# Partition sums of the modulation values: fp32 products with one column of ones, or high and low parts in fp32r with two columns

## The chip, the cores and the metric

The kernel runs on one core of one Trainium2 chip. The metric is device time in microseconds of one execution. A version's time is the median of its runs.

## The reference, cut to what matters

The reference is two transformer blocks in a row on 512 tokens of width 1024. The first has attention (eight heads with a forget gate, eight with dilated windows) and a layer of 16384 small experts; the second has a retention branch, a convolution branch and a gated feed-forward layer. The second block is modulated by a vector `c`:

```
cs = jax.nn.silu(c)
mod = cs @ ada_w[l] + ada_b[l]                    # 1024 -> 6 * 1024
sh_m, sc_m, gt_m, sh_f, sc_f, gt_f = jnp.split(mod, N_MOD, axis=-1)
h = modulate(rmsnorm(x, norm_mix_g[l]), sh_m, sc_m)
```

The change touches only how the six vectors of 1024 values in `mod` are summed.

## The kernel before, in words

**Layout.** Activations are kept with features on the 128 partitions, as 8 chunks of 128 features by 512 tokens. Weights come from memory as fp32 chunks of 128 by 1024 (512 KB).

**Projections.** A projection chunk (`wload`, lines 140 to 147, and `mm3`, lines 149 to 153) works in three products. ACT copies the weight chunk into the format fp32r (line 145, tile `wh`, the high part), DVE or POOL subtracts that from the fp32 chunk (line 146, tile `wl`, the low part), and TensorE runs high times high, high times low and low times high (lines 151, 152, 153), each with 512 or 256 columns of activations. The tags `wh` and `wl` have three buffers each in a pool that lives through the whole kernel, so a new high part waits until TensorE is done with the chunk three before it.

**The modulation values.** `ada(j)` (line 245) makes one of the six vectors. Eight weight rows of 128 by 1024 are multiplied by a value per partition and added into the fp32 tile `acc` (name `ada`): the first on ACT (line 259), four on DVE (line 261), the last three scaled on ACT (line 263) and added on POOL (line 264). `ada_sum` (line 270) then sums over partitions: for each of 8 blocks of 128 columns, `acc` is the stationary operand and one column of fp32 ones is the moving one (line 274), the result lands in one column of the PSUM tile `adaps`, and DVE adds `ada_b` and writes `mod` (line 276). For j of 0 to 3 the sum follows at once; for j of 4 and 5 it is put off to `after` (line 368), which is called between the two halves of the output projection's last chunks (`resid`) and behind them.

**The order of the work.** In this stage no order is written out by hand: a scheduler orders each engine's instructions by the place in the program and by when it expects operands and buffers to be ready, and the engines then run that order with semaphores. The loop over `c` in `attention` emits the q and k projections of the next pair of heads, the heads of this pair (`heads`, ending in the transposes `mt` of line 449) and then `ada(c - 1)`. Behind `attention` come the queries of the expert layer (`queries`, `proj_halves`): three weight chunks of `wq` are split into high and low parts, the low ones on POOL, and their products start with the first 256 tokens, going through the three chunks for each k. From there to the end of the expert layer the order is written by hand.

Of the kernel before, what the change touches and what calls it, by code (L numbers as in the profile page):

```python
# [11 lines left out]
F32R = mybir.dt.float32r  # L12
# [3 lines left out]
AF = mybir.ActivationFunctionType  # L16
OP = mybir.AluOpType
# [3 lines left out]
D = 1024  # L21
# [37 lines left out]
def f32(ap):  # L59
    return ap.bitcast(F32)  # L60
# [39 lines left out]
class Builder:  # L100
# [113 lines left out]
    def consts(self):  # L214
        nc, a, c = self.nc, self.a, self.const
        self.hT = self.big.tile([128, KD, T], F32, name="hT")
        self.xh = self.big.tile([128, KD, T], F32R, name="xh")
        self.xl = self.big.tile([128, KD, T], F32R, name="xl")
        self.xt = self.big.tile([128, D], F32, name="xt")
        nc.vector.memset(self.xt[:, :T // 2], 0.0)  # L220
        self.blank = self.xt[:, :T // 2].bitcast(BF16)
        self.mean_w = c.tile([128, 1], F32, name="mean_w")
        nc.vector.memset(self.mean_w, 1.0 / D)
        self.vec = c.tile([128, a["vecs"].shape[1]], F32, name="vec")
        nc.scalar.dma_start(self.vec, a["vecs"])
        self.ones1 = c.tile([128, 1], F32, name="ones1")
        nc.vector.memset(self.ones1, 1.0)
        o = self.a["vec_off"]
        self.v = {n: self.vec[:, o[n]:o[n] + w] for n, w in self.a["vec_w"].items()}

# [38 lines left out]

    def ada_sum(self, j, acc):  # L270
        nc = self.nc
        p = self.bank("pt", "adaps")
        for m in range(8):
            nc.tensor.matmul(p[:, m:m + 1], lhsT=acc[:, m * 128:m * 128 + 128], rhs=self.ones1,
                             start=True, stop=True)
        nc.vector.tensor_tensor(self.mod[:, j * 8:j * 8 + 8], p[:, 0:8],
                                self.v["ada_b"][:, j * 8:j * 8 + 8], OP.add)
        if j == 5:
            self.gs = self.const.tile([128, 16], F32, name="gs")
            for i, (g, sc) in enumerate((("norm_mix_g", 1), ("norm_ffn_g", 4))):  # L280
                nc.vector.scalar_tensor_tensor(self.gs[:, i * 8:i * 8 + 8], self.mod[:, sc * 8:sc * 8 + 8], 1.0,
                                               self.v[g], op0=OP.add, op1=OP.mult)
# [1117 lines left out]
```

## Time and profile before

| What | Value |
|---|---|
| median of 3 runs | 2491.91 us (2490.35 to 2492.84) |
| the profiled execution's own time | 2493.93 us |
| span in its profile | 2492.0 us |
| TensorE busy | 2458.2 us, 99% of the span |
| VectorE (DVE) busy | 1714.6 us |
| ScalarE (ACT) busy | 938.9 us |
| GpSimd (POOL) busy | 623.3 us |
| mean granted TensorE clock | 0.995 |

The span is what the profiler sees of one execution; the execution's own time is 1.93 us longer. Matmul records overlap, because the next one starts while the last drains: the distance from one start to the next tells what a matmul takes from TensorE, not its duration. An fp32 matmul of these sums leaves two records, each with a weight load of its own; an fp32r matmul leaves one.

### The profile page before, as it was taken

The page shows a single profiled execution, that of the slowest core. Times are in us where ns is not written, and L with a number is a line of the kernel's source. Part 1 is how long each engine was busy: PE and PEld are TensorE (multiplying, and loading weights), DVE is VectorE, ACT ScalarE, POOL GpSimd, SP SyncE. Part 2 cuts the span into 40 slices and gives each one's busy share as a digit, 9 for nine tenths or more (in the row PEclk, how much of TensorE's full clock was granted, in tenths as well). Part 3 has the DMA queues.
Part 4 walks back from the last instruction along what each step waited for, and adds up shares of the span by engine and source line. Part 5 has one row for each costly group of instructions (what it writes and reads, how often), then busy time and mean ns, then how long its engine had stood idle before and what let it go on. Part 6 is the DMA issues. An engine that isn't in the chain of part 4 may idle for free.

```text
span 2492.0 us, 34252 instructions
## 1 busy us (share of the span) xinstructions
PE 2458.2 (99%) x12881; PEld 2135.9 (86%) x12881; DVE 1714.6 (69%) x3224; ACT 938.9 (38%) x1401; POOL 623.3 (25%) x460
## 2 busy tenths in 40 slices
PE   9999999999999999999999999999999999999998
PEld 7788889999999999999888887777888888888887
DVE  5767589898885998889888885877543336433333
ACT  5667244444554333333333334411223223322221
POOL 1132146670002666566543320000000001000000
PEclk9999999999999999999999999999999999999999
DMA  4476224455777999999999982422232322232332
GB/s 168 146 244 223 76 82 135 157 174 187 263 266 275 399 376 370 371 369 387 370 383 383 380 295 96 132 85 85 85 102 94 102 93 93 86 101 93 97 94 64
DMA packets 191285, 496.99 MB, mean 199 GB/s; under 512 B 16136, under 2 KB 85384, under 8 KB 189584
## 3 DMA queue, kind: packets, MB, share of 16 engines
q1 hardware_dynamic: 142352, 322.02, 38.5%
q0 software_dynamic: 36864, 134.23, 14.2%
q10 hardware_dynamic: 11904, 38.56, 4.0%
q8 instruction: 101, 1.65, 0.3%
q14 instruction: 64, 0.52, 0.1%
HBM read 455.48 MB, written 39.27 MB: 199 GB/s over the span
## 4 chain that ended last, share of the span: by engine, by line
PE 94%; DVE 2%; ACT 2%; DMA 1%; issue 0%; ACTq 0%; SPq 0%; POOL 0%; DVEq 0%
PE up L151 7%; PE up L153 7%; PE up L152 7%; PE oacc L966 7%; PE oacc L965 7%; PE oacc L964 7%; PE fg L152 2%; PE fg L153 2%; PE fg L151 2%; PE fd L151 2%; PE fd L153 2%; PE fd L152 2%; PE q L151 2%; PE q L152 2%; PE fu L152 2%; PE fu L151 2%
## 5 line engine op out<-in xcount | busy, mean ns | idle before, releaser
L145 ACT ACTIVATE wh<-ws 128x1024 fp32r<-128x1024 f32 (+2 forms) x206 | 214.7, 1043 | 659.7 <-issue 228.5
L146 DVE TENSOR_TENSOR wl<-ws,wh 128x1024 fp32r<-128x1024 f32 (+2 forms) x200 | 240.8, 1204 | 254.6 <-ACT wh L145 253.1
L884 ACT ACTIVATE wh<-ws 128x1024 fp32r<-128x1024 f32 x269 | 284.5, 1058 | 227.6 <-issue 78.2
L888 DVE TENSOR_TENSOR wl<-ws,wh 128x1024 fp32r<-128x1024 f32 x231 | 285.7, 1237 | 105.3 <-ACT wh L884 102.7
L151 PE MATMUL up<-xh,wh 128*128 128x384 f32 x1024 | 346.6, 338 | 1.3 <-ACT gel L918 1.3
L153 PE MATMUL up<-xh,wl 128*128 128x384 f32 x1024 | 343.8, 336 | 0.3 <-DVE wl L888 0.3
L152 PE MATMUL up<-xl,wh 128*128 128x384 f32 x1024 | 343.3, 335 | 0.0
L966 PE MATMUL oacc<-wh,al 128*128 128x512 f32 x768 | 300.1, 391 | 0.0
L965 PE MATMUL oacc<-wl,ah 128*128 128x512 f32 x768 | 300.0, 391 | 0.0
L964 PE MATMUL oacc<-wh,ah 128*128 128x512 f32 x768 | 299.2, 390 | 0.0
L970 POOL DMA_INDIRECT row<-in_peer_u,eidx x128 | 182.6, 1427 | 324.4 <-DMA ws<-in_u_blk 195.2
L970 POOL DMA_INDIRECT row<-in_peer_v,eidx x128 | 188.1, 1470 | 210.3 <-DVE acc L996 189.0
L918 ACT ACTIVATE gel<-up 128x384 f32<-128x384 f32 x128 | 63.0, 492 | 409.3 <-PE up L153 409.3
L151 PEld LDWEIGHTS up<-xh,wh 128*128 128x128 f32 x1024 | 192.7, 188 | 3.6 <-ACT gel L918 1.6
L152 PEld LDWEIGHTS up<-xl,wh 128*128 128x128 f32 x1024 | 192.9, 188 | 2.0
L153 PEld LDWEIGHTS up<-xh,wl 128*128 128x128 f32 x1024 | 192.7, 188 | 0.9 <-DVE wl L888 0.6
L966 PEld LDWEIGHTS oacc<-wh,al 128*128 128x128 f32 x768 | 144.1, 188 | 29.8
L965 PEld LDWEIGHTS oacc<-wl,ah 128*128 128x128 f32 x768 | 144.1, 188 | 29.0
L964 PEld LDWEIGHTS oacc<-wh,ah 128*128 128x128 f32 x768 | 144.2, 188 | 28.5
L996 DVE SCALAR_TENSOR_TENSOR acc<-row,wg,acc 128x1024 f32<-128x1024 f32 x127 | 162.5, 1280 | 1.0
L985 DVE CUSTOM_DVE_ANT_0 scr<-row,xt 128x1024 bf16<-128x1024 f32 x128 | 156.3, 1221 | 5.5 <-DMA row<-in_peer_u,eidx 3.7
L146 POOL TENSOR_TENSOR wl<-ws,wh 128x1024 fp32r<-128x1024 f32 x6 | 14.4, 2402 | 567.8 <-ACT wh L145 567.8
(375 smaller groups left out, 5329.2 us busy)
## 6 DMA issues: line engine op xcount, KB each, us to landing
ws<-in_u_blk SPq DMA_DIRECT2D x128, 512.0 KB, 3.9
ws<-in_v_blk SPq DMA_DIRECT2D x128, 512.0 KB, 9.2
ws<-in_w_t SPq DMA_DIRECT2D x64, 512.0 KB, 3.3
ws<-in_ada_w SPq DMA_DIRECT2D x48, 512.0 KB, 4.6
gates_d<-gst ACTq DMA_DIRECT2D x12, 2048.0 KB, 7.0
gr<-gates_d SPq DMA_DIRECT2D x32, 768.0 KB, 10.6
gel_d<-gel ACTq DMA_DIRECT2D x61, 192.0 KB, 2.8
gel<-gel_d SPq DMA_DIRECT2D x61, 192.0 KB, 8.1
```

The costliest lines, as they stand in the source:

```text
L145: nc.scalar.activation(wh, ws, AF.Copy)
L146: (low or nc.vector).tensor_tensor(wl, ws, f32(wh), OP.subtract)
L151: mm(out, lhsT=wh, rhs=xh, start=first, stop=False)
L152: mm(out, lhsT=wh, rhs=xl, start=False, stop=False)
L153: mm(out, lhsT=wl, rhs=xh, start=False, stop=last)
L884: self.nc.scalar.activation(x["wh"], x["ws"], AF.Copy)
L888: eng.tensor_tensor(x["wl"], x["ws"], f32(x["wh"]), OP.subtract)
L964: mm(o, lhsT=ah[:, t], rhs=vh[:, d], start=j == 0, stop=False)
L965: mm(o, lhsT=ah[:, t], rhs=vl[:, d], start=False, stop=False)
L966: mm(o, lhsT=al[:, t], rhs=vh[:, d], start=False, stop=j == 127)
L970: self.nc.gpsimd.indirect_dma_start(out=u, out_offset=None, in_=self.a["peer_v" if i >= 128 else "peer_u"], in_offset=bass.IndirectOffsetO ...
L996: nc.vector.scalar_tensor_tensor(self.acc, u, self.wg[:, j:j + 1], self.acc, op0=OP.mult, op1=OP.add)
```

## The change

A tile `ones2` of 128 by 2 in fp32r is made once from the fp32 ones. `ada_sum` splits `acc` into a high part on ACT (a buffer of the tag `wh`) and a low part on DVE (a buffer of the tag `wl`), and for each of the 8 blocks runs two matmuls, high and low, each with two columns of ones, that accumulate in PSUM. The PSUM tile has two columns for each block, of which the first is read.

```diff
         self.ones1 = c.tile([128, 1], F32, name="ones1")
         nc.vector.memset(self.ones1, 1.0)
+        self.ones2 = c.tile([128, 2], F32R, name="ones2")
+        nc.scalar.activation(self.ones2, self.ones1.to_broadcast([128, 2]), AF.Copy)
...
     def ada_sum(self, j, acc):
         nc = self.nc
-        p = self.bank("pt", "adaps")
+        p = self.bank("pt", "adaps", (128, 8, 2))
+        hi = self.w.tile([128, D], F32R, tag="wh", bufs=3, name="wh")
+        nc.scalar.activation(hi, acc, AF.Copy)
+        lo = self.w.tile([128, D], F32R, tag="wl", bufs=3, name="wl")
+        nc.vector.tensor_tensor(lo, acc, f32(hi), OP.subtract)
         for m in range(8):
-            nc.tensor.matmul(p[:, m:m + 1], lhsT=acc[:, m * 128:m * 128 + 128], rhs=self.ones1,
-                             start=True, stop=True)
-        nc.vector.tensor_tensor(self.mod[:, j * 8:j * 8 + 8], p[:, 0:8],
+            for x in (hi, lo):
+                nc.tensor.matmul(p[:, m], lhsT=x[:, m * 128:m * 128 + 128], rhs=self.ones2,
+                                 start=x is hi, stop=x is lo)
+        nc.vector.tensor_tensor(self.mod[:, j * 8:j * 8 + 8], p[:, :, 0],
                                 self.v["ada_b"][:, j * 8:j * 8 + 8], OP.add)
```

## Rows read from the trace of the kernel before

**Rows 1.** The page: busy time, and the chain that ended last, by engine.

```profile
PE 2458.2 (99%) x12881; PEld 2135.9 (86%) x12881; DVE 1714.6 (69%) x3224; ACT 938.9 (38%) x1401; POOL 623.3 (25%) x460
...
PE 94%; DVE 2%; ACT 2%; DMA 1%; issue 0%; ACTq 0%; SPq 0%; POOL 0%; DVEq 0%
```

**Rows 2.** By tile, adaps: the sums' weight loads, ns min/median/max, first and last start.

```profile
L274 PEld LDWEIGHTS adaps<-ones,ada x96: 190/192/192, 122.5 to 300.4; 128*128 128x128 f32 x96
```

**Rows 3.** By tile, mod: its reader in the norms of the second block.

```profile
L294 ACT ACTIVATE xh<-y,mod x32: 492/496/511, 1525.5 to 2127.6; 128x256 fp32r<-128x256 f32 x32
```

**Rows 4.** Timeline of PE around the first sum: start, us, operation.

```profile
122.58 1.84 PE L274 MATMUL adaps<-ones,ada 128*128 128x1 f32 x16
124.28 0.48 PE L152 MATMUL q<-xl,wh 128*128 128x512 f32 x1
124.60 0.39 PE L153 MATMUL q<-xh,wl 128*128 128x512 f32 x1
124.83 0.40 PE L151 MATMUL q<-xh,wh 128*128 128x512 f32 x1
```

**Rows 5.** Stretches: busy of PE, PEld, DVE, ACT, POOL; clock, DMA share, GB/s.

```profile
300.00:305.00 5.00, 5.00 (x32) 5.00 (x32) 4.25 (x19) 1.57 (x4) 2.72 (x3) 0.66 0.44 131
80.00:240.00 160.00, 152.74 (x938) 129.16 (x937) 114.38 (x238) 108.98 (x227) 49.20 (x30) 0.99 0.68 225
```

**Rows 6.** Timeline of PE at the end of the output projection, and the queries' start.

```profile
289.71 0.28 PE L153 MATMUL res<-mixh,wlast 128*128 128x256 f32 x1
289.83 1.84 PE L274 MATMUL adaps<-ones,ada 128*128 128x1 f32 x16
291.54 0.36 PE L151 MATMUL res<-mixh,wlast 128*128 128x256 f32 x1
...
298.86 1.84 PE L274 MATMUL adaps<-ones,ada 128*128 128x1 f32 x16
300.57 0.58 PE L92 MATMUL st<-mean_w,sq 128*128 128x1 f32 x4
301.01 0.36 PE L151 MATMUL q<-xh,wh 128*128 128x256 f32 x1
```

**Rows 7.** Timeline of ACT at the start, where the new constant joins.

```profile
4.30 0.21 ACT L250 ACTIVATE cs<-vec 128x8 f32<-128x8 f32 x1 [1.83 <-DMA vec<-in_vecs]
```

**Rows 8.** Timeline of PE: fp16 products of 128 columns, later in the kernel.

```profile
603.23 0.22 PE L803 MATMUL gp<-o,o 128*128 128x128 f16 x1
603.29 0.22 PE L802 MATMUL gp<-o,o 128*128 128x128 f16 x1
```

**Rows 9.** Groups by line, 80 to 240 us: count, busy us, mean ns, idle before.

```profile
L146 DVE TENSOR_TENSOR wl<-ws,wh 128x1024 fp32r<-128x1024 f32 x13 | 15.9, 1222 | 0.2 <-ACT wh L145 0.2
L145 ACT ACTIVATE wh<-ws 128x1024 fp32r<-128x1024 f32 x13 | 13.5, 1047 | 0.0
...
L151 PEld LDWEIGHTS q<-xh,wh 128*128 128x128 f32 x48 | 9.1, 189 | 3.4 <-ACT ks L397 1.7 <-ACT wh L145 0.4
...
L424 PEld LDWEIGHTS <-identb 128*128 128x128 bf16 x31 | 3.3, 105 | 2.6 <-issue 1.8
```

**Rows 10.** Timeline of POOL: an add for the first sum, a later weight split.

```profile
113.48 2.38 POOL L264 TENSOR_TENSOR ada<-ada,ws 128x1024 f32<-128x1024 f32 x1
...
283.56 2.40 POOL L146 TENSOR_TENSOR wl<-ws,wh 128x1024 fp32r<-128x1024 f32 x1 [3.04 <-ACT wh L145]
```

**Rows 11.** Timeline of ACT: idle behind the first sum; copies of the queries' weights.

```profile
127.77 0.59 ACT L389 ACTIVATE qh<-q 64x512 fp32r<-64x512 f32 x1 [4.39 <-PE q L153]
...
271.59 1.06 ACT L145 ACTIVATE wh<-ws 128x1024 fp32r<-128x1024 f32 x1 [3.90 <-issue]
...
282.42 1.06 ACT L145 ACTIVATE wh<-ws 128x1024 fp32r<-128x1024 f32 x1 [3.80 <-PE res L152]
```

**Rows 12.** Timeline of PE: products of the queries behind the last sum.

```profile
301.73 0.41 PE L152 MATMUL q<-xl,wh 128*128 128x256 f32 x1
301.95 0.41 PE L153 MATMUL q<-xh,wl 128*128 128x256 f32 x1
```

## The prediction

> **What bounds the kernel now.** The page comes first: TensorE is busy for 2458.2 of 2492.0 us and holds 94% of the chain that ended last [rows 1]. So a step costs or gives time only through what TensorE itself does, or through a wait of TensorE that nothing else fills. By tile, the sums have 96 records, two for each of 48 fp32 matmuls, each with its weight load, in six groups from 122.5 to 300.4 us [rows 2]. The timeline of TensorE tells what one group takes: in the tail of the attention stage it starts at 289.83 and the next product at 291.54, so 1.71 us, or 0.107 us a record [rows 6]; at 122.58 it is 1.70 [rows 4]. All six are 10.3 us. No reader hurries: the norms of the second block read `mod` from 1525.5 us on [rows 3]. The stretch from 80 to 240 us, with the heads of attention and the first four sums, shows TensorE busy for 152.74 of 160 us, DVE for 114.38, ACT for 108.98 [rows 5]: it has 7.3 us of waits and some slack beside it. [...]
>
> **The constant.** One ACT operation on 128 by 2 elements, like the 0.21 us one on 128 by 8, which itself came after 1.83 us of waiting for a DMA [rows 7]. That wait hides it: 0, at most +0.2.
>
> **The matmuls.** 48 fp32 matmuls with two records each become 96 fp32r matmuls with one record each: the count of weight loads is the same. With one or two columns there is nothing to stream, so I take the load as what paces them, at 0.107 us as now: 0. No row has fp32r below 256 columns, so the price is bounded. At the 0.12 us of fp32r with 256 columns [rows 6], 16 times 0.013 for six groups is +1.2. At the 0.06 us of fp16 products [rows 8], a group takes 0.96, and six save 4.5. If a short fp32r product ran in two passes as fp32 does, 32 records of 0.107 are 3.42 a group, +10.3 in all. I stay at 0, because a load in fp32r is recorded with 189 ns, near the 192 of fp32 [rows 2] and far from the 105 of bf16 [rows 9]. Behind an fp32 group the second fp32r product starts 0.32 us after the first, not 0.23 [rows 4]: 0.09 for the change of format. Four groups stand behind transposes of fp32 data, where this only moves; one has fp32r on both sides: -0.1, between -0.5 and 0.
>
> **The splits of the first four sums.** Each adds a copy on ACT (1047 ns) and a subtraction on DVE (1222 ns) [rows 9]: 4.2 and 4.9 us, 9.1 if nothing hid them. The matmuls now wait for the low part, and behind them in TensorE's order stand q products; behind the copy on ACT the next head's `qh`, behind the subtraction on DVE the next `ada` and `ql`. But the first sum's last POOL add ends at 115.9 [rows 10] and its matmuls start at 122.58 [rows 4]: 6.7 us for 2.3 us of splitting. ACT then idles 4.39 us before `qh` [rows 11]. What fails to hide I take from the stage's own leak: 7.3 of 160 us is 4.6%, and 4.6% of 9.1 is +0.4. Both ends: +9.1, and -1.5 if the order, which the scheduler makes anew, happens to close some of the 7.3 us of waits. If this cover is gone, TensorE is late with q and k, and then with the next scores. SP issues no new DMA; POOL's own operations are unchanged.
>
> **The splits of the last two sums.** Here the buffers decide. `wh` has three. In the tail ACT takes one each time TensorE finishes a chunk: the three query chunks are copied from 271.59 to 282.42, the first and last of three [rows 11]. In program order the parts for j = 4 and 5 come before the query chunks, so they should take the buffers at 271.6 and 277, and keep them until their matmuls are done: 291.5 and 300.6 [rows 6]. The first query chunk is then copied at 282.4, the second at 291.6, the third at 300.6. That one is ready in its low part at about 300.6 + 1.06 + 2.40 [rows 10, 11] = 304.1, or some 0.8 later behind POOL's norm work, while the products start at 301.01 [rows 6] and reach the third chunk six products later, about 302.3, its low part at 302.7 (0.22 each [rows 12]). In strict order TensorE waits 1.4 to 2.2 us; if the scheduler runs the other two chunks first, 48 products cover it. I take +0.8. Upper end: 2.2 and one more stretch at the lower clock, which costs 5 times 0.34, or 1.7, by the granted clock of 300 to 305 us [rows 5]: +3.9. Lower end: the stretch at the lower clock goes, because the last sum moves away from `st`: -1.7. The POOL queue is the one moved: its subtraction lands among the norm's.
>
> **The sum.** 0 - 0.1 + 0.4 + 0.8 = +1.1 us on the profiled execution's 2493.93 (span 2492.0 and 1.93 around it): 2495.0. That execution lies 2.0 above the median of the runs shown, so on the median 2491.91 I give **2493.0 us**. A measurement of this kernel can tell about 0.2%, 5 us, from no change; this is no change.
>
> **The rivals.**
>
> *The short product in two passes* (slower). Place: TensorE, all six groups. It costs +10.3 beyond my sum, 2503.3. It decides from a group length of about 2.4 us on (six times 0.7 is over 4). For it: no row shows fp32r below 256 columns, so none speaks of such a short product. Against it: every fp32r product here has one record. Chance 0.08.
>
> *The splits stay on the chain of the heads* (slower): the low part is late at all four sums, TensorE stands still behind it, and the scores after it move; up to +9.1 in place of +0.4, 2501.7, and over 5 from about half of that on. For it: DVE is 71% busy there. Against it: 6.7 us of lead. Chance 0.10.
>
> *The query chunks wait for the sums' buffers in strict order*: +3.9 in place of 0.8, 2496.1, still no change. For it: three buffers and the program's order. Against it: 48 products to run first. Chance 0.14.
>
> *A fast load* (faster): the fp32r loads go at 0.06 and save 4.5, so 2488.5; with the low stretch gone as well, 2486.8. For it: the fp16 rows. Against it: 189 ns against 105 [rows 9]. Chance 0.08, half of it faster by over 5 us. [...]
>
> **How the numbers follow.** The main case has 0.60, its own bounds 2489 to 2497. Faster by over 5 us: half of the fast load and a little of the main case's low end, 0.07. Slower by over 5: the two passes 0.08, the heads 0.09, the tail and a bad order 0.04: 0.21. The rest, 0.72, is no change. The range runs from 2488.0 (the fast load with the splits) to 2500.0 (the heads half exposed); above it lie the two passes and the worst of the heads, below it a fast load with luck.
>
> **What the new profile would show.** Right: `adaps` as 96 records of two columns, a group still 1.7 to 1.9 us; copies for j = 4 and 5 on ACT near 272 and 277, and the second and third query chunks copied near 292 and 301; TensorE's busy share from 80 to 240 us within a microsecond of 152.74. Wrong: groups of 3.4 or of 1.0 us; idle time of TensorE before `adaps` ended by the low part; query copies still in front of 283; the clock of 300 to 305 us back at 1.0, or a second low stretch.

## The result, and the profile after

The changed kernel takes **2505.01 us** (median of six runs, 2502.54 to 2508.37) against 2492.35 for the kernel before (six runs, 2490.35 to 2493.93): ratio 1.0053 [1.0043, 1.0063], slower by 12.7 us. The prediction was 2493.0, and its range ended at 2500.0. The profiled execution is the slowest of the six (2508.37, span 2506.3), so its stretches add up to 14.3 us, 1.6 more than the medians differ by.

The page of the kernel after, busy time and the chain by engine:

```profile
PE 2463.0 (98%) x12881; PEld 2140.8 (85%) x12881; DVE 1720.5 (69%) x3230; ACT 945.7 (38%) x1409; POOL 617.8 (25%) x460
...
PE 93%; DVE 2%; ACT 2%; DMA 1%; issue 1%; POOL 1%; SPq 0%; ACTq 0%; DVEq 0%; POOLq 0%
```

Next to [rows 1] TensorE has the same 12881 instructions and is busy 4.8 us longer, and the span grew by 14.3: most of the loss is idle time, the rest is the same work done more slowly. First the suspects of the prediction. By tile, the loads of the sums after (ns min/median/max, first and last start):

```profile
L281 PEld LDWEIGHTS adaps<-ones,wh x48: 190/192/333, 122.6 to 311.7; 128*128 128x128 f32 x48
L281 PEld LDWEIGHTS adaps<-ones,wl x48: 192/192/333, 122.7 to 311.8; 128*128 128x128 f32 x48
```

96 loads at a median of 192 ns, as in [rows 2]. TensorE's timeline after, around the group of the sum for j = 4:

```profile
300.25 0.17 PE L281 MATMUL adaps<-ones,wh 128*128 128x2 f32 x1
...
301.96 0.36 PE L151 MATMUL res<-mixh,wlast 128*128 128x256 f32 x1
302.16 0.28 PE L152 MATMUL res<-mixl,wlast 128*128 128x256 f32 x1
```

From the group's start to the next product it is 1.71 us, as before [rows 6]. The matmuls cost what the old ones cost, and the loss is elsewhere. To place it I used two landmarks of TensorE's timeline: the transposes `mt` that end each head, and the spread of `half`, which ends the tail of the attention stage (starts in us). From here on "head" followed by a number is one turn of the loop over `c`, which holds a pair of heads; turns 4 to 7 are the dilated ones.

| landmark | before | after | moved by |
|---|---|---|---|
| `mt`, head 0 | 109.28 | 109.24 | 0.0 |
| `mt`, head 2 | 147.50 | 148.41 | 0.9 |
| `mt`, head 3 | 174.47 | 178.93 | 4.5 |
| `mt`, head 4 | 196.62 | 204.57 | 8.0 |
| `mt`, head 7 | 254.94 | 264.43 | 9.5 |
| spread of `half` | 311.20 | 324.77 | 13.6 |
| end of the span | 2492.0 | 2506.3 | 14.3 |

So there are two losses: **9.5 us in the heads** (head 0 to head 7: 145.66 us before, 155.19 after) and **4.1 us in the tail** (head 7 to the spread: 56.26 before, 60.34 after). The landmark of head 7 is not a clean cut, because products of the output projection are mixed in before it: behind it stand 120 products `res` of 512 columns before and 124 after (rows of lines 151 to 153), 0.23 us each. So 0.9 us of the tail's 4.1 is work that has only changed sides, and the losses are nearer to 10.4 and 3.2. The stretches after (columns as in [rows 5]):

```profile
80.00:240.00 160.00, 147.66 (x876) 125.10 (x875) 110.70 (x220) 102.97 (x207) 44.88 (x29) 0.96 0.62 209
```

TensorE is busy for 147.66 us where [rows 5] has 152.74, and its mean granted clock is 0.96 instead of 0.99.

**The heads.** The timeline of the engines around the second sum (j = 1) after, start and duration in us, in brackets the idle time and what ended it:

```profile
135.96 4.82 POOL L266 TENSOR_TENSOR ada<-ada,ws 128x1024 f32<-128x1024 f32 x2
...
138.26 0.19 ACT L437 ACTIVATION_READ_ACCUMULATOR e<-e,m 128x1 f32 x1
...
140.81 1.06 ACT L276 ACTIVATE wh<-ada 128x1024 fp32r<-128x1024 f32 x1 [2.37 <-POOL ada L266]
...
141.78 0.47 ACT L445 ACTIVATE pts<-pt 128x384 f32<-128x384 f32 x1
...
142.30 1.44 PE L447 MATMUL o<-v,pts 128*128 128x64 f32 x11 [2.05 <-ACT pts L445]
```

The new copy (L276) stands on ACT between an exponential of head 2 and that head's next `pts`. ACT has nothing to do from 138.4 on, but the copy at the head of its queue waits for POOL's last addition, which ends at 140.78. Behind the copy waits `pts`, and behind `pts` TensorE: 2.05 us. ACT keeps to its order here: the 0.47 us copy of `pts` starts at 141.78, behind the new one of 140.81, though the last transposes `pt` before it had ended by 139.65. At the third sum the same happens:

```profile
162.09 4.83 POOL L266 TENSOR_TENSOR ada<-ada,ws 128x1024 f32<-128x1024 f32 x2
...
166.95 1.06 ACT L276 ACTIVATE wh<-ada 128x1024 fp32r<-128x1024 f32 x1 [2.46 <-POOL ada L266]
...
168.66 0.90 PE L440 MATMUL pt<-ident,e 128*128 128x128 f32 x3 [2.15 <-ACT e L437]
```

A third stall has another cause. TensorE's timeline at the first scores of head 5, and the waits from 100 to 330 us (total, times, longest, in us), both after:

```profile
200.90 0.38 PE L428 MATMUL s<-ks,qh 128*128 128x256 f32 x1 [1.51 <-DVE m L435]
```

```profile
ACT wh L145 <- PE adaps L281: 6.7, 2, 4.3
ACT wh L276 <- POOL ada L266: 5.4, 3, 2.5
...
DVE e L435 <- DMA bias<-in_k_dil: 2.3, 1, 2.3
```

There VectorE waited for the bias of a dilated head, which SP issued only at about 195 us, behind two `ada_w` loads. And behind the second and the third of these stalls TensorE's clock falls (stretches of 4 us, columns as in [rows 5]):

```profile
168.00:172.00 4.00, 3.34 (x17) 3.34 (x18) 3.63 (x7) 3.44 (x9) 0.00 (x0) 0.58 0.59 199
172.00:176.00 4.00, 4.00 (x21) 3.81 (x21) 1.16 (x6) 3.20 (x7) 0.00 (x0) 0.57 0.60 190
200.00:204.00 4.00, 3.10 (x16) 2.74 (x17) 3.29 (x6) 1.54 (x3) 0.00 (x0) 0.85 0.10 24
204.00:208.00 4.00, 4.00 (x24) 3.66 (x24) 0.89 (x3) 0.60 (x1) 0.00 (x0) 0.73 0.93 373
```

In the kernel before every stretch of 4 us from 100 to 300 us has 1.00. These four lose 4 times (0.42 + 0.43 + 0.15 + 0.27) = 5.1 us of full clock. With the stalls, 2.05 + 2.15 + 1.51 = 5.7, that makes 10.8 at most (a stall inside one of these stretches is counted twice), enough for the 9.5 to 10.4.

**The tail.** ACT's timeline after, the copies alone:

```profile
282.01 1.06 ACT L276 ACTIVATE wh<-ada 128x1024 fp32r<-128x1024 f32 x1 [3.91 <-PE res L152]
...
287.45 1.06 ACT L276 ACTIVATE wh<-ada 128x1024 fp32r<-128x1024 f32 x1 [3.86 <-PE res L152]
...
292.83 1.06 ACT L145 ACTIVATE wh<-ws 128x1024 fp32r<-128x1024 f32 x1 [3.79 <-PE res L152]
...
302.02 1.06 ACT L145 ACTIVATE wh<-ws 128x1024 fp32r<-128x1024 f32 x1 [4.26 <-PE adaps L281]
...
312.01 1.06 ACT L145 ACTIVATE wh<-ws 128x1024 fp32r<-128x1024 f32 x1 [2.42 <-PE adaps L281]
```

The parts for j = 4 and 5 take two of the three `wh` buffers, and the query chunks, which were copied by 282.42 before [rows 11], come at 292.83, 302.02 and 312.01. TensorE's timeline shows the two waits that this ends in:

```profile
307.80 0.43 PE L210 MATMUL spread<-ident,n 128*128 128x128 f32 x2 [1.09 <-DVE n L201]
...
314.04 0.60 PE L92 MATMUL st<-mean_w,sq 128*128 128x1 f32 x4 [1.95 <-ACT sq L86]
```

The second is ACT's queue again: `sq` stands behind the query copy of 312.01, which waited for `adaps`. The first is VectorE, whose operations stretched while POOL made the low parts of these late chunks. The timelines of POOL and of DVE after:

```profile
303.16 2.39 POOL L146 TENSOR_TENSOR wl<-ws,wh 128x1024 fp32r<-128x1024 f32 x1 [6.79 <-ACT wh L145]
...
313.14 2.37 POOL L146 TENSOR_TENSOR wl<-ws,wh 128x1024 fp32r<-128x1024 f32 x1 [2.73 <-ACT wh L145]
```

```profile
304.33 1.25 DVE L195 TENSOR_SCALAR n<-n 128x2 int32<-128x2 int32 x1
...
313.40 2.39 DVE L309 TENSOR_TENSOR xl<-y,xh 128x256 fp32r<-128x256 f32 x1 [1.11 <-ACT xh L307]
...
316.88 0.41 DVE L309 TENSOR_TENSOR xl<-y,xh 128x256 fp32r<-128x256 f32 x1
317.22 0.16 DVE L195 TENSOR_SCALAR n<-n 128x2 int32<-128x2 int32 x1
```

The operations that take 0.16 and 0.41 us later take 1.25 and 2.39 here, and they end at 305.58 and 315.79, where POOL's end at 305.55 and 315.51.

### The profile page after: what moved, and what is told of

Its sections match the earlier page's. It is cut to its first block, busy times and chain, and to the rows that moved or that the text cites. A ratio compares the mean times of both kernels' runs of the same rounds, so it can differ in the third digit from the quotient of the medians.

```text
span 2506.3 us, 34260 instructions
## 1 busy us (share of the span) xinstructions
PE 2463.0 (98%) x12881; PEld 2140.8 (85%) x12881; DVE 1720.5 (69%) x3230; ACT 945.7 (38%) x1409; POOL 617.8 (25%) x460
## 4 chain that ended last, share of the span: by engine, by line
PE 93%; DVE 2%; ACT 2%; DMA 1%; issue 1%; POOL 1%; SPq 0%; ACTq 0%; DVEq 0%; POOLq 0%
PE up L151 7%; PE up L153 7%; PE up L152 7%; PE oacc L973 7%; PE oacc L972 7%; PE oacc L971 7%; PE fg L152 2%; PE fg L153 2%; PE fg L151 2%; PE q L152 2%; PE q L151 2%; PE fd L151 2%; PE q L153 2%; PE fd L153 2%; PE fd L152 2%; PE fu L152 2%
```

## The experiments

Of all of them two lengths are compared, read from the profiles as above: **heads** (head 0 to head 7) and **tail** (head 7 to the spread of `half`). Ratios are against the kernel before on the same chip (median 2491.3 for the first eight, 2492.7 for the next four, 2491.6 for the last three). Each length comes from one profile, and in it head 7's landmark moves: behind it stand 112 (`e7_both_bias`) to 124 `res` products of 512 columns, so up to 2 us can belong to the other length.

**Taking the two losses apart.** `e1_own` gives the last two sums' parts other buffers:

```
-        hi = self.w.tile([128, D], F32R, tag="wh", bufs=3, name="wh")
...
+            hi = [self.tmp.tile([128, T], F32R, tag="e", bufs=4, name="mh") for _ in range(2)]
+            lo = [self.tmp.tile([128, T], F32R, tag=t, bufs=3, name="ml") for t in ("pts", "bias")]
```

> The parts for j = 4 and 5 take other buffers (the idle e, pts and bias tiles of the heads, in halves of 512 columns), so the three query chunks get their wh and wl buffers as before; the first four sums are left as changed. Theory A (the copy of the high part waits for POOL at the head of ACT's queue in the heads, and the query chunks wait for the sums' buffers in the tail): the tail's some 4 us go, the heads' some 9 stay, 8.5 to 10 us above the kernel before. Theory B (only the added ACT and DVE work costs, wherever its buffers are): 12 to 13 above. Theory C (the order was merely shuffled, no place is to blame): anything, most likely 10 to 14 above.

`e2_defer` emits each of the first four sums one head later, at the start of the next `ada`; `e3_both` has both edits:

```
+        if self.pend is not None:
+            self.ada_sum(*self.pend)
...
-            self.ada_sum(j, acc)
+            self.pend = (j, acc)
```

> The first four sums are emitted one head later, with the same operations and the same buffers, so that acc has long been done when its high part is copied. Theory A: ACT no longer stands still for POOL, TensorE's waits of 2 us in the heads and the low clock behind them go, and some 9 of the 12.7 us with them: 3 to 5 us above the kernel before, the rest being the tail. Theory B: the same work is still there, 12 to 13 above. Theory C: 8 to 14 above.

> Both together: sums one head later, other buffers in the tail. Theory A: nothing is left but the splits themselves, 0 to 2 us above the kernel before. Theory B: 12 to 13 above. Theory C: 6 to 14 above.

`e4_pool` lets POOL make both parts, buffers and place unchanged:

```
-        nc.scalar.activation(hi, acc, AF.Copy)
+        nc.gpsimd.tensor_copy(hi, acc)
...
-        nc.vector.tensor_tensor(lo, acc, f32(hi), OP.subtract)
+        nc.gpsimd.tensor_tensor(lo, acc, f32(hi), OP.subtract)
```

> The high and the low parts of all six sums are made on POOL, right behind its own last add, in the same wh and wl buffers. Theory A: no copy can block ACT or DVE, the heads are as before if POOL's copy and subtraction (2.4 us each at most, by its rows) end before the sums' place in TensorE's order: 3 to 5 us above the kernel before, from the tail, or up to 3 more where POOL is late. Theory B: ACT and DVE have no work added, 0 to 2 above. Theory C: 5 to 14 above.

| | us | ratio | heads | tail |
|---|---|---|---|---|
| before | | | 145.66 | 56.26 |
| after | 2505.01 | 1.0053 [1.0043, 1.0063] | 155.19 | 60.34 |
| e1_own | 2502.30 | 1.0047 [1.0030, 1.0064] | 155.47 | 54.77 |
| e2_defer | 2503.32 | 1.0044 [1.0028, 1.0061] | 153.71 | 61.27 |
| e3_both | 2497.94 | 1.0033 [1.0022, 1.0045] | 147.31 | 56.29 |
| e4_pool | 2500.14 | 1.0033 [1.0021, 1.0044] | 150.80 | 61.38 |

The tail is settled by this: with buffers of their own it is as short as before, with the ring's it stays at 60 to 61. The times are 11.0, 12.1, 6.7 and 8.9 us above the kernel before, all four beyond what theory A expected (8.5 to 10, 3 to 5, 0 to 2, and 3 to 5 or up to 3 more). In the heads the wait for POOL is gone in the last three, and yet time is lost: 8.1 us in `e2_defer` and 5.1 in `e4_pool`. In `e3_both` the profile shows only 1.7, but the execution that it shows took 2491.06 us, where the seven have a median of 2497.94 and go up to 2502.05; so the 6.7 us of the median are in no profile. The mean granted clock of that execution was 0.997, that of the two of 2502 us 0.993. In `e2_defer`, TensorE's timeline and the waits from 100 to 260 us:

```profile
195.33 0.91 PE L451 MATMUL o<-v,pts 128*128 128x64 f32 x6 [2.50 <-DVE pts L447]
```

```profile
DVE e L439 <- DMA bias<-in_k_dil: 11.2, 4, 4.3
```

VectorE now waits four times for the bias that cost one stall after; in `e3_both` it waits four times too, 8.8 us in all. Those loads stand on SP's queue among the `ada_w` loads, which wait for their own buffers (in `e2_defer` 31.6 us for DVE's and 27.2 for POOL's operations of `ada`), and every new order of the stage puts them elsewhere. That made a second theory: the loss in the heads is SP's order, not ACT's copy. From here on the expectations call the copy's wait theory A and SP's order theory B.

**Which of the two causes is first.** `e5_nosplit` keeps the two columns and the wider PSUM tile, and has no parts; the other three move the dilated heads' bias to another queue, in the changed kernel, in `e3_both` and in the kernel before:

```
-            for x in (hi, lo):
-                nc.tensor.matmul(p[:, m], lhsT=x[:, m * 128:m * 128 + 128], rhs=self.ones2,
...
+            nc.tensor.matmul(p[:, m], lhsT=acc[:, m * 128:m * 128 + 128], rhs=f32(self.ones2),
```

```
-                nc.sync.dma_start(b, a["k_dil"][:, h])
+                nc.scalar.dma_start(b, a["k_dil"][:, h])
```

> The sums keep two columns of ones and the wider PSUM tile, but the high and low parts are left out: one float32 matmul per 128 columns, as before. If the parts (their copy, their subtraction, their buffers) are the whole cause, this is the kernel before again: head 7's transposes end at 254 to 256 us and the time is 2490 to 2494. If the new shape of the sums or a mere shuffle of the order of instructions costs, some of the loss stays: 2497 or more.

> The changed kernel, with the bias loads of heads 4 to 7 issued from ScalarE's queue, so that they don't stand behind ada_w loads on SP's. If ScalarE's copy waiting for the last POOL addition is what costs the heads (theory A), the three waits of 2 to 3 us at c = 1 to 3 stay and with them head 7's end at 260 us or later, in all 2499 to 2505. If the order of SP's loads is the cause (theory B), the waits for the bias go, head 7 ends before 259 and the time falls to 2499 or less.

> First four sums one head later, buffers of their own for the last two, and the bias loads of heads 4 to 7 on ScalarE's queue. The same kernel without the last edit took 2497.9, with waits of VectorE for the bias of 3 to 4 us. If those loads behind SP's ada_w loads are what is left of the loss (theory B), the waits go, head 7 ends at 254 or earlier and the time is 2487 to 2492, no slower than before. If not (the splits' work on ScalarE and VectorE itself is late, theory C), it stays at 2495 to 2499.

> The kernel before with only the bias loads of heads 4 to 7 on ScalarE's queue, to price that move by itself. Before had no wait for that bias in its heads, so both theories expect no change: 2490 to 2494. If it is faster by over 3 us, the move helps by itself and the run of all three edits must be judged against this one; if slower, loads on ScalarE's queue hold up its exponentials.

| | us | ratio | heads | tail |
|---|---|---|---|---|
| e5_nosplit | 2492.02 | 1.0000 [0.9991, 1.0009] | 145.63 | 54.80 |
| e6_after_bias | 2506.67 | 1.0062 [1.0046, 1.0077] | 156.52 | 58.94 |
| e7_both_bias | 2492.09 | 1.0002 [0.9993, 1.0011] | 147.16 | 54.48 |
| e8_before_bias | 2491.40 | 0.9998 [0.9989, 1.0007] | 145.63 | 56.33 |

Without parts nothing is lost. In the changed kernel the bias's queue alone saves nothing (2506.67 lies above even theory A's 2499 to 2505): no wait for the bias is left in its heads, but the copies wait 2.18 and 2.25 us and the heads stay long. Once the copy is out of the way (`e7_both_bias`), the queue takes away what was left, and the whole loss is recovered with all parts and matmuls in place. That step is read from the times, 2497.94 to 2492.09: in the profiles (that of `e3_both` shows its execution of 2491.06 us) the heads hardly differ (147.31 and 147.16), while the waits for the bias fall from 8.8 us to 1.0. By itself the move is worth nothing. So the copy comes first, and the bias is what is late next.

**The copy, the subtraction, the place.** `e10_pool_own_bias` is `e1_own` with the bias moved and the first four sums' parts on POOL; `e12_own_bias` is the same with the parts left on ACT and DVE; `e11_hi_twice` is the changed kernel without the low part of the first four:

```
+        lo = hi
+        if j >= 4:
...
-            for x in (hi, lo):
+            for i, x in enumerate((hi, lo)):
```

> The first four sums' parts made by GpSimd, right behind its own last addition, so that neither ScalarE's nor VectorE's queue waits for GpSimd; buffers of their own for the last two, bias on ScalarE's queue; the sums not put off. If the loss in the heads is ScalarE's copy waiting at the head of its queue (theory A), it is gone: head 7 ends at 252 to 257 and 2488 to 2493. If it is the parts' later arrival at TensorE, or the crowded order, it stays: 2497 or more.

> The changed kernel, where the first four sums leave out the low part: VectorE's subtraction is gone and the high part is multiplied twice, so TensorE has the same 16 matmuls. ScalarE's copy stays. Theory A (the copy at the head of ScalarE's queue): its waits of 2 to 3 us for GpSimd stay, head 7 ends at 260 to 265, and 2499 to 2506. If VectorE's subtraction, of 1 us and waiting for the copy, is what costs the heads: head 7 ends before 258 and 2497 or less.

> Buffers of their own for the last two sums and the bias on ScalarE's queue; the first four sums made where the changed kernel makes them. Theory A: the waits of the copy stay and cost the heads 8 to 10 us against the kernel of all three edits, in all 2498 to 2503, as with the own buffers alone (2502.3). If the bias loads were the main cause in the heads: 2495 or less.

| | us | ratio | heads | tail |
|---|---|---|---|---|
| e10_pool_own_bias | 2492.83 | 0.9996 [0.9986, 1.0005] | 147.96 | 55.42 |
| e11_hi_twice | 2497.95 | 1.0020 [1.0011, 1.0029] | 146.19 | 59.85 |
| e12_own_bias | 2503.53 | 1.0045 [1.0030, 1.0061] | 155.65 | 56.06 |

`e10` and `e12` differ only in who makes the parts of the first four sums: 147.96 against 155.65, and 2492.83 against 2503.53, just above the 2498 to 2503 expected. `e11` fits neither of its expectations whole: the heads are short, though ACT still copies. ACT's timeline there shows why:

```profile
138.64 1.05 ACT L276 ACTIVATE wh<-ada 128x1024 fp32r<-128x1024 f32 x1
...
163.16 1.05 ACT L276 ACTIVATE wh<-ada 128x1024 fp32r<-128x1024 f32 x1
...
189.09 1.06 ACT L276 ACTIVATE wh<-ada 128x1024 fp32r<-128x1024 f32 x1 [1.46 <-POOL ada L266]
```

Without the subtraction the scheduler made another order, in which two of the copies find their sum ready. With `e7_both_bias`, where copies and subtractions all stand in the heads and nothing is lost, this says that it is not the copy's 1.06 us that costs, but a long wait of it for POOL; in `e7_both_bias` three of the copies wait 1.03 us for TensorE, and that costs nothing. This run can't tell whether the subtraction has a share of its own, so two more were made on the kernel before, with its old matmuls: `e13_copy` adds only the copy, `e14_parts` copy and subtraction, for the first four sums; nothing reads them.

```
+        if j < 4:
+            hi = self.w.tile([128, D], F32R, tag="wh", bufs=3, name="wh")
+            nc.scalar.activation(hi, acc, AF.Copy)
```

> The kernel before, with its float32 matmuls, and beside the first four sums ScalarE's copy of the sum alone, which nothing reads. If a copy that waits for GpSimd ahead of the heads' exponentials is enough (theory A), head 7 ends at 260 to 265 and the time is 2498 to 2503 wherever the trace shows the copies waiting 2 us or more; where their place in the queue falls so late that they wait under 1 us, there is no loss: 2490 to 2493. A loss without such waits, or such waits without a loss, is against theory A.

> The kernel before, with its float32 matmuls, and beside the first four sums both parts, copy and subtraction, which nothing reads. As in the changed kernel the heads should lose 8 to 11 us if the copies wait 2 us or more for GpSimd (theory A), in all 2498 to 2503, and nothing if they don't. If the new matmuls have a share in the loss of the heads, it is clearly under 8 with the same waits.

They took 2502.13 us, ratio 1.0042 [1.0027, 1.0057], heads 154.04, tail 57.19; and 2506.85, 1.0061 [1.0046, 1.0077], heads 158.70, tail 56.98; the second lies above its expectation. **One unread copy per sum loses 8.4 us in the heads.** The timeline of `e13_copy` around its fourth:

```profile
182.15 7.30 POOL L264 TENSOR_TENSOR ada<-ada,ws 128x1024 f32<-128x1024 f32 x3 [15.95 <-ACT ws L263]
...
186.80 0.19 ACT L433 ACTIVATION_READ_ACCUMULATOR e<-e,m 128x1 f32 x1
...
189.48 1.06 ACT L275 ACTIVATE wh<-ada 128x1024 fp32r<-128x1024 f32 x1 [2.48 <-POOL ada L264]
190.56 0.59 ACT L400 ACTIVATE ks<-k 64x512 fp32r<-64x512 f32 x1
191.18 0.49 ACT L441 ACTIVATE pts<-pt 128x384 f32<-128x384 f32 x1
...
191.72 1.55 PE L443 MATMUL o<-v,pts 128*128 128x64 f32 x12 [2.88 <-ACT pts L441]
```

Part of the 8.4 is again the bias (VectorE waits 4.8 us for it), which no run took out of this kernel. Counted over all kernels: in the six where a copy waits 2 us or more for POOL (after, e1, e6, e12, e13, e14) the heads take 154.0 to 158.7 us; in those where none does, 145.6 to 148.0, but for e2 and e4, whose late bias showed.

**Where TensorE's own time decides.** Two runs with the parts and the ones in fp16: `e9_fp16` is `e7_both_bias` with all six sums so; `e15_tail_fp16` is the kernel before with only the last two sums so, in buffers of their own.

```
...
+            hi = self.tmp.tile([128, D], FP16, tag="e", bufs=4, name="mh")
+            lo = self.tmp.tile([128, D], FP16, tag="pts" if j < 5 else "bias", bufs=3, name="ml")
...
```

> The kernel of all three edits (sums one head later, buffers of their own, bias on ScalarE's queue; 2492.1), with the parts and the ones in fp16, all twelve parts in the tags e, pts and bias. Its 16 matmuls a sum should follow one another at 0.06 us, as the bf16 and fp16 products of this kernel do, where float32r takes 0.11: about 0.8 us less a sum, 4.8 in all. If TensorE's own time decides in the heads, 2486 to 2489; if the chain beside it does, or if the parts in the heads' own buffers bring waits, no change or more: 2491 to 2496.

> The kernel before for the first four sums; the last two in fp16 parts in buffers of the tags e, pts and bias. In the run with fp16 everywhere 16 such matmuls took 0.55 us where the float32 ones take 1.7, and behind the heads TensorE works without a break, so two sums save 2 to 2.5 us: 2488 to 2490.5. If the loss of theory A reaches these two sums as well, or their parts come late: 2492 or more.

`e9_fp16` took 2490.14 us, between its two expectations, 0.9992 [0.9983, 1.0001], heads 147.31, tail 53.02; `e15_tail_fp16` 2488.85, **0.9989 [0.9980, 0.9998]**, heads 145.84, tail 52.55. TensorE's timeline of the second at the sum for j = 4:

```profile
287.76 0.18 PE L286 MATMUL adaps<-ones,mh 128*128 128x2 f16 x1
287.80 0.16 PE L286 MATMUL adaps<-ones,ml 128*128 128x2 f16 x1
287.83 0.16 PE L286 MATMUL adaps<-ones,mh 128*128 128x2 f16 x1
...
288.18 0.36 PE L151 MATMUL res<-mixh,wlast 128*128 128x256 f32 x1
```

The stretches of `e15_tail_fp16` (columns as in [rows 5]):

```profile
240.00:305.00 65.00, 63.26 (x428) 56.25 (x427) 39.97 (x86) 24.40 (x44) 11.20 (x8) 1.00 0.21 69
305.00:370.00 65.00, 64.31 (x371) 56.77 (x370) 52.92 (x264) 29.03 (x48) 31.10 (x31) 1.00 0.28 89
```

Sixteen matmuls take 0.42 us instead of 1.71. In the heads these 1.29 us a sum bought nothing (147.31 against 147.16 in `e7_both_bias`): TensorE isn't what limits them. In the tail two sums give 2.6, and a new wait of 0.63 for `sq` stands against it: 2.0. The profile's tail is 3.7 shorter (56.26 to 52.55). Two more `res` products stand before its landmark (0.5), and the stretch at the lower clock behind the last sum is missing, which was worth 5 times 0.34 = 1.7 [rows 5]; with these the sum is 4.2. That stretch is missing in `e1_own` and `e5_nosplit` as well (tails 54.77 and 54.80, clock 1.00), without fp16, so it is not shown that the fp16 sums took it away. The median is 2.8 us below that of the kernel before; the interval leaves out 1, but the gain is under the 0.2% that count here as a change.

## Why the prediction was wrong

- **The constant and the matmuls** were right, but for the -0.1 for the change of format: behind the fp32r group the second product still starts 0.20 us after the first (301.96 and 302.16), as behind the fp32 group (291.54 [rows 6] and 291.74), and not 0.12 as between the others. Head 0 ends where it did, and the group in the tail takes 1.71 us. The rival of two passes (groups of 3.4) and that of a fast load (1.0) fell with that.
- **"The splits of the first four sums"** is the step that failed: +0.4 taken, +9.5 measured (nearer 10.4 with the `res` products that changed sides). Its cover was the 6.7 us between POOL's last addition and TensorE's use of the first sum. But the copy isn't placed when TensorE needs it. It stands in ACT's fixed order near the moment the sum is expected, and what it can hold up is all that stands behind it there: the scores' exponentials. Measured at that place the cover was not 6.7 us but less than nothing: -0.60, -2.37 and -2.46 at the first three sums, and only the fourth sum was ready. The prediction itself named `qh` behind the copy and then did not ask how long the copy would wait. The leak of 4.6% had nothing to do with it; the late bias and the low clock came on top.
- The rival **"the splits stay on the chain of the heads"** (up to +9.1, chance 0.10) has the right size by luck: another mechanism gave it. It had TensorE waiting for the low part; TensorE never did. It waited for head 2's `pts` and head 3's `e`.
- **"The splits of the last two sums"** named the mechanism and was off in size: +0.8 taken, +4.1 measured between the landmarks, of which 0.9 are the four products that changed sides; the 3.2 left lie under its upper end of 3.9. The copies came where it said (282.01, 287.45, 302.02 and 312.01; less the 9.5 us of the heads, 272.5, 278.0, 292.5 and 302.5). The hope that 48 other products cover the third chunk left out that the waiting copy holds up `sq` on ACT (TensorE waits 1.95 us for it) and that VectorE's norms stretched while POOL's late subtractions ran (0.16 to 1.25 us, 0.41 to 2.39). The two waits of TensorE are 3.0 us, against 0.17 before; the low stretch moved to 312 to 320 us (granted clock 0.93 and 0.65 in its halves) and costs 4 times 0.42 = 1.7, as the one before did [rows 5]; of the remaining 1.2 the four products are 0.9. The step's lower end (-1.7) took the lower clock for an effect of the last sum next to `st`. That was the author's estimate, and no run shows it: in the changed kernel the last sum's last matmul starts at 311.83 and `st` at 314.04, and the low stretch came all the same.
- The two upper ends together, 9.1 + 3.9, are 13.0, and the medians differ by 12.7. That they agree so well is luck, since the first came from another mechanism. But the text had a loss at both places, as rivals that exclude each other; they are independent, and both losses came.

Open is why the order leaves the copy about one POOL addition (2.4 us) too early. That the scheduler expects POOL to be faster than it is would fit, but no run tested it. The subtraction's own share is open too: `e14_parts` loses 4.7 us more in the heads than `e13_copy`, with its copies in other places. And why the executions of `e3_both` differ by 11 us is not shown, beyond the clocks listed with them.

## What to carry to other kernels

An operation put on a queue can cost its wait as well as its duration, and what stands behind it pays (here a copy of 1.06 us waited 2.37 us for POOL, and TensorE 2.05 us behind it): look for the lead at the place where it stands in that queue, not at the place where its result is used. Where a producer is slow and just in time, let the producer's own engine do the follow-up work (`e10_pool_own_bias`), or put it off until the data is surely there (`e7_both_bias`). Here both needed the bias on another queue as well: in `e4_pool` and `e2_defer`, without it, the bias came late. A shared ring of buffers is a queue as well: here two long holders in a ring of three set the pace of what runs through it (the last query chunk was copied at 312.01 us, against 282.42 before [rows 11]).

## What the runs showed of the hardware that wasn't expected

- Sixteen fp16 matmuls of two columns (`e15_tail_fp16`), each with its own load of 128 columns recorded at 95 ns, started 0.025 us apart, less than half of the 0.06 that the fp16 products of 128 columns [rows 8] let one expect; in fp32r (the changed kernel) the same took 0.11.
- Two of VectorE's operations stretched to the end of a running POOL subtraction (0.16 to 1.25 us, 0.41 to 2.39): both started after POOL's and ended 0.03 and 0.28 us after it. One has two inputs (line 309), the other one (line 195); the one of 0.16 us at 304.13 (line 194) ran beside the first of the two subtractions without stretching. No run shows why.
- Idle time was not the whole price of a stall: behind two of the three stalls in the heads the granted clock was 0.57 to 0.85 in two stretches of 4 us each, which cost 5.1 us of full clock, almost as much as the 5.7 us of all the stalls. Behind the first stall it stayed at 1.00.
